# Laying SBUF out anew: stationary tiles beside the constants, weights and work tiles at the other end

## The chip, the cores and the metric

The program runs on one core of one Trainium2 chip. The metric is the device time of one execution in microseconds (us), the median of the runs shown. TensorE does the matrix products, VectorE (DVE), ScalarE (ACT) and GpSimd (POOL) the rest, and DMAs that SyncE (SP) issues bring the weights from HBM into SBUF, the on-chip memory of 128 partitions. A matrix product reads two operands from SBUF: the stationary one (128 columns here) is loaded into the array by an instruction of its own, the moving one (up to 512 columns) is streamed past it. The result goes to PSUM.

## The reference

A decoder of two layers on x of 256 tokens x 1024 channels, all in float32. Each layer does

```
x = x + 0.5 * ((silu(a) * b) @ wo),  a, b = split(rms_norm(x, g) @ wi)      # FFN 1, D_FF = 2816
h = rms_norm(x, g);  z = h @ w_in                                          # queries, keys, values, gates
y = sum over 3 attentions of sigmoid(gate_i) * (o_i @ P_i)                 # stick-breaking, latent, sparse
x = x + y @ w_out
x = x + 0.5 * swiglu_ffn(x)                                                # FFN 2
```

The three attentions have eight heads of width 64 each. Every weight is used once for all 256 tokens, so each is read from HBM once.

## The kernel before

**Products.** The tokens are two tiles of 128 (t = 0, 1). Activations are transposed and are the stationary operand, 128 x 128 at a time; the weights are the moving operand, 512 columns at a time (256 and 440 in a few places). To keep float32 accuracy each operand is split in a high and a low part (`split`, lines 524 to 526), and `mm3` (lines 528 to 532) does three products for one: high x high (L530), high activation x low weight (L531), low activation x high weight (L532). The granted names in the trace read `acc<-whi,hThi`: first the moving, then the stationary tile.

**Stages.** `ffn` runs over six column chunks of a and b (the first of 256, five of 512; eight blocks of 128 in depth, both t, three products each), with hT as the stationary operand; then `out_rows` multiplies gT (silu(a)*b transposed; 22 blocks, both t, both halves of the 1024 output columns) by wo. `mixer` does the input projections with hT, the attentions, the merges with the attention outputs oT (`oh`, `ol`) as the stationary operand, and ends in `out_rows` with yT, which lies in hT's slots, times w_out. By these loops one FFN has 480 products of 512 columns and 96 of 256 on hT and 264 on gT; one mixer 528 of 512, 48 of 440 and 48 of 256 columns on hT, 144 on oT, 36 on the latent vectors cT, and 96 on yT.

**Order.** TensorE executes in the order in which the program is written. In the mixer the order of TensorE, VectorE and ScalarE is worked out by a planner (`Planner`, with costs written by hand) before the program is emitted. Elsewhere the framework schedules VectorE, ScalarE and the DMAs. Weights come in slabs: a DMA into `raw` (six buffers), a ScalarE copy to `whi` (L514, in the mixer L817), a VectorE subtraction to `wlo` (L515, L819); four slabs are held.

**Memory.** A tile pool takes its tiles from SBUF in the order of opening, one behind the other in every partition; a pool that closes gives its place to the next one. All four pools `cp` (constants), `sm`, `wp` (weights), `hp` (hT and the large work tiles "hy": x, h, y, mq, mk, nq, nk) lie on the left side, and behind them in turn `fp` (an FFN's gT) and `mp` (a mixer's tiles). Added up from the tile sizes (a tile is rounded up to 32 bytes), in KB of one partition counted from the kernel's first tile:

| tiles | before | after the change |
| --- | --- | --- |
| constants and small tiles; in them zkh, zkl at 8.2 to 10.7 | 0 to 24.9 | 0 to 24.9 |
| whi, wlo, raw | 24.9 to 40.9, to 56.9, to 68.9 | the last 44 KB, from the far end |
| hy, six tiles of 4 KB | 68.9 to 92.9 | the 24 KB before these |
| hThi, hTlo (two of each) | 92.9 to 100.9, to 108.9 | 24.9 to 32.9, to 40.9 |
| FFN: gh0, gl0, gh1, gl1, 11 KB each | 109.0 to 153.0 | 41.0 to 85.0 |
| mixer: V0, V1, then cT/zw | 109.0 to 125.0, to 133.0 | 41.0 to 57.0, to 65.0 |
| mixer: oh, ol | 139.5 to 147.5, to 155.5 | 65.0 to 73.0, to 81.0 |
| mixer: wr (moving operand of the value products) | 194.2 to 206.2 | 126.2 to 138.2 |

`g_col` in `cp` has 32 bytes, so that before the change the weights, hT, gT, oT and wr all start 32 bytes off a multiple of 64 bytes.

Of the kernel before, what the change touches and what calls it, by code (L numbers as in the profile page):

```python
# [345 lines left out]
W_BUFS = 4  # L346
# [10 lines left out]
def decoder_trunk(ctx, tc, x_in, wts, gains, lcon, cst, out, depth=DEPTH):  # L357
# [3 lines left out]

    cp = ctx.enter_context(tc.tile_pool(name="cp", bufs=1))
    sm = ctx.enter_context(tc.tile_pool(name="sm", bufs=5))
    wp = ctx.enter_context(tc.tile_pool(name="wp", bufs=W_BUFS))
    hp = ctx.enter_context(tc.tile_pool(name="hp", bufs=2))
    dp = ctx.enter_context(tc.tile_pool(name="dp", bufs=1, space=bass.MemoryType.DRAM))
    pb = ctx.enter_context(tc.tile_pool(name="pb", bufs=8, space=PSUM))
    ctx.enter_context(tc.manual_schedule(engines={nc.tensor.engine}))
# [8 lines left out]
        return pb.tile([128, 512], F, tag="ps", name="att")  # L377

    def big_tile(name, dt=F, shape=(128, D)):
        return hp.tile(list(shape), dt, tag="hy", name=name, bufs=6)  # L380

    A = slice(None)

# [5 lines left out]
    for t in range(NT):  # L389
        xs.append(big_tile("x"))  # L390
# [13 lines left out]


    g_row = big_tile("grow")[0:8, 0:128]
    nc.sync.dma_start(g_row, gains[0].rearrange("(k p) -> k p", k=8))
    g_col = cp.tile([128, 8], F, name="g_col")
# [11 lines left out]
    def load_consts():  # L420
        nc.sync.dma_start(ct, cst[:, RW + 128:])
        rf = big_tile("rf")
        nc.sync.dma_start(rf[:, :RW], cst[:, :RW])
        nc.vector.tensor_copy(rt, rf[:, :RW])
# [314 lines left out]
    def mixer(l):  # L739
# [26 lines left out]
        def new_oT():  # L766
            return (mp.tile([128, 4, S], R, tag="oh", name="oh", bufs=2),
                    mp.tile([128, 4, S], R, tag="ol", name="ol", bufs=2))
# [14 lines left out]
        def events(*n):  # L783
            return [events(*n[1:]) for _ in range(n[0])] if n else event()
# [87 lines left out]

        cT = mp.tile([128, 2, NT, 3, 128], R, tag="r3", name="cT")
        cT = cT[:, 0], cT[:, 1]
        krg = [mp.tile([128, 56], F, name=f"krg{t}") for t in range(NT)]
        ev_hT, ev_rn, ev_cT, ev_krg = events(2), [Tok(2.0), Tok(4.0)], events(NT), events(NT)

# [208 lines left out]
        side = {"_uq": side_uq, "_ukv": side_ukv, "w1_slab": lambda: compress()}  # L1086
# [105 lines left out]
                yield from merge(c, *gs[c], o_nsa, ev_onsa, False, final=True)  # L1192


        o_sb, o_mla, o_nsa = new_oT(), new_oT(), new_oT()
        ev_osb, ev_omla, ev_onsa = events(4), events(4), events(4)
        ev_sbpv, ev_sbm = event(), event()

# [318 lines left out]
        def compress():  # L1517

            c = done_c[0]
            done_c[0] += 1  # L1520
            for s in range(2):
                i = take()
                k = yield "P", 1.0, 1.2, (ev_zw, *slab_ev[i]), () if s else (s_acc,)
                if not s:
                    a = acc_tile()
                sl = slabs[i][1]
                for j in range(8):
                    jj = s * 8 + j
                    js = slice(j * 128, (j + 1) * 128)
                    if jj:  # L1530
                        nc.tensor.matmul(a[:M, 0:128], zw[:, c, jj, 0:M], sl[1][:, js], start=False, stop=False)
                    nc.tensor.matmul(a[:32 + M, 0:128], zw[:, c, jj, 0:32 + M], sl[0][:, js],
                                     start=jj == 0, stop=jj == 15)
                    if not jj:
                        nc.tensor.matmul(a[:M, 0:128], zw[:, c, jj, 0:M], sl[1][:, js], start=False, stop=False)
                s_w.put(k)
                mark()
            spawn(hidden(c, a, k), 0.0)
# [252 lines left out]
    for l in range(depth):  # L1791
        ffn(l, 0)
        mixer(l)
        ffn(l, 2)
# [33 lines left out]
```

## Time and profile before

| what | us |
| --- | --- |
| median of 3 runs | 1328.75 (1328.41 to 1329.15) |
| the profiled execution's own time | 1328.05 |
| its span in the profile | 1326.3 |
| TensorE busy in it | 1302.1 |
| VectorE busy | 893.9 |
| ScalarE busy | 796.4 |

In the profile TensorE's products are pipelined and their ends are modelled: one starts before the one ahead of it is shown as ended, and the busy time of a stretch does not tell how fast they follow each other. The views that list instructions in order of time give each one's start; the difference of two starts, divided by the number of products between them, is the spacing that counts for the time. "PEclk" is the TensorE clock that was granted, 1.00 or a digit 9 for its upper level of 2.4 GHz, half for 1.2 GHz.

### The profile page before, as it was taken

The page shows a single profiled execution, that of the slowest core. Times are in us where ns is not written, and L with a number is a line of the kernel's source. Part 1 is how long each engine was busy: PE and PEld are TensorE (multiplying, and loading weights), DVE is VectorE, ACT ScalarE, POOL GpSimd, SP SyncE. Part 2 cuts the span into 40 slices and gives each one's busy share as a digit, 9 for nine tenths or more (in the row PEclk, how much of TensorE's full clock was granted, in tenths as well). Part 3 has the DMA queues.
Part 4 walks back from the last instruction along what each step waited for, and adds up shares of the span by engine and source line. Part 5 has one row for each costly group of instructions (what it writes and reads, how often), then busy time and mean ns, then how long its engine had stood idle before and what let it go on. Part 6 is the DMA issues. An engine that isn't in the chain of part 4 may idle for free.

```text
span 1326.3 us, 19987 instructions
## 1 busy us (share of the span) xinstructions
PE 1302.1 (98%) x6623; PEld 1078.1 (81%) x6623; DVE 893.9 (67%) x1852; ACT 796.4 (60%) x1654; POOL 43.4 (3%) x50
## 2 busy tenths in 40 slices
PE   7999999999899999999999999999989999999998
PEld 6888888888777888888888888888878778888887
DVE  6655557988997775555466554679879876755553
ACT  5545447796888555454464544478868884645442
POOL 0000000210000000000000000011100000000000
PEclk9999999999999999999999999999999999999999
DMA  7765557545434656555656565565453356565563
GB/s 226 245 190 177 189 179 219 181 127 175 128 90 135 184 174 198 189 183 183 191 179 216 178 190 181 188 217 160 133 173 110 102 159 176 173 191 183 183 189 112
DMA packets 124504, 230.77 MB, mean 174 GB/s; under 512 B 13928, under 2 KB 15600, under 8 KB 124400
## 3 DMA queue, kind: packets, MB, share of 16 engines
q1 hardware_dynamic: 124144, 228.97, 55.5%
q8 instruction: 52, 0.85, 0.3%
q0 software_dynamic: 256, 0.52, 0.1%
q14 instruction: 52, 0.43, 0.1%
HBM read 225.77 MB, written 3.15 MB: 173 GB/s over the span
## 4 chain that ended last, share of the span: by engine, by line
PE 85%; ACT 7%; DVE 6%; issue 2%; DMA 0%; SPq 0%; ACTq 0%; DVEq 0%
PE acc L530 26%; PE acc L532 26%; PE acc L531 26%; ACT wf L1340 2%; ACT whi L817 2%; PE tp L692 1%; DVE wlo L819 1%; ACT wf L1367 1%; DVE wr L1384 1%; DVE wlo L515 1%; DVE x L626 1%; PE att L1290 1%; PE att L1726 1%; PE att L1262 1%; DVE wf L1350 0%
## 5 line engine op out<-in xcount | busy, mean ns | idle before, releaser
L515 DVE TENSOR_TENSOR wlo<-raw,whi 128x512 fp32r<-128x512 f32 (+1 forms) x560 | 361.9, 687 | 318.0 <-ACT whi L514 316.6
L514 ACT ACTIVATE whi<-raw 128x512 fp32r<-128x512 f32 (+1 forms) x560 | 323.0, 623 | 374.7 <-PE acc L532 366.4
L530 PE MATMUL acc<-whi,hThi 128*128 128x512 f32 (+2 forms) x1248 | 480.3, 385 | 0.5 <-ACT hThi L525 0.5
L532 PE MATMUL acc<-whi,hTlo 128*128 128x512 f32 (+2 forms) x1248 | 470.4, 377 | 0.6 <-DVE hTlo L526 0.6
L531 PE MATMUL acc<-wlo,hThi 128*128 128x512 f32 (+2 forms) x1248 | 469.0, 376 | 0.0
L532 PEld LDWEIGHTS acc<-whi,hTlo 128*128 128x128 f32 x1248 | 235.3, 189 | 44.6 <-DVE hTlo L526 1.0
L530 PEld LDWEIGHTS acc<-whi,hThi 128*128 128x128 f32 x1248 | 235.7, 189 | 39.5 <-ACT hThi L525 1.0
L531 PEld LDWEIGHTS acc<-wlo,hThi 128*128 128x128 f32 x1248 | 235.9, 189 | 37.7
L819 DVE TENSOR_TENSOR wlo<-raw,whi 128x512 fp32r<-128x512 f32 (+1 forms) x276 | 181.4, 681 | 42.2 <-ACT whi L817 40.6
L817 ACT ACTIVATE whi<-raw 128x512 fp32r<-128x512 f32 (+1 forms) x276 | 162.9, 618 | 53.9 <-PE acc L532 42.4
L530 PE MATMUL acc<-whi,gh 128*128 128x512 f32 x352 | 140.1, 398 | 0.0
L532 PE MATMUL acc<-whi,gl 128*128 128x512 f32 x352 | 139.0, 395 | 0.0
L531 PE MATMUL acc<-wlo,gh 128*128 128x512 f32 x352 | 139.0, 395 | 0.0
L532 PEld LDWEIGHTS acc<-whi,gl 128*128 128x128 f32 x352 | 66.1, 188 | 15.9
L531 PEld LDWEIGHTS acc<-wlo,gh 128*128 128x128 f32 x352 | 66.2, 188 | 15.3
L530 PEld LDWEIGHTS acc<-whi,gh 128*128 128x128 f32 x352 | 66.1, 188 | 15.3
L537 POOL TENSOR_TENSOR rs<-ss,mh 128x1 f32<-128x1 f32 (+4 forms) x30 | 36.6, 1223 | 1034.0 <-DVE ss L536 1012.6
L1340 ACT ACTIVATE wf<-wf,mn 128x128 f32<-128x128 f32 x96 | 42.7, 446 | 12.1 <-DVE mn L1350 11.7
L530 PE MATMUL acc<-whi,oh 128*128 128x512 f32 x96 | 41.2, 429 | 0.5 <-DVE y L1155 0.5
L532 PE MATMUL acc<-whi,ol 128*128 128x512 f32 x96 | 39.1, 408 | 0.0
L531 PE MATMUL acc<-wlo,oh 128*128 128x512 f32 x96 | 39.1, 407 | 0.0
L683 DVE SCALAR_TENSOR_TENSOR g<-acc,rn,sil 128x512 f32<-128x512 f32 (+1 forms) x48 | 33.6, 703 | 2.9 <-PE acc L532 0.8
(274 smaller groups left out, 1262.6 us busy)
## 6 DMA issues: line engine op xcount, KB each, us to landing
raw<-in_wts SPq DMA_DIRECT2D x824, 256.0 KB, 2.7
gain<-in_gains SPq DMA_DIRECT2D x5, 512.0 KB, 5.7
xd<-x SPq DMA_DIRECT2D x4, 512.0 KB, 4.4
x<-xd SPq DMA_DIRECT2D x4, 512.0 KB, 4.1
raw<-in_wts SPq DMA_DIRECT2D x8, 184.0 KB, 2.5
lc<-in_lcon SPq DMA_DIRECT2D x2, 528.0 KB, 7.5
x<-in_x SPq DMA_DIRECT2D x4, 256.0 KB, 5.3
out_dram<-x SPq DMA_DIRECT2D x4, 256.0 KB, 2.0
```

The source lines that it names most:

```text
L514: nc.scalar.activation(hi[:, c:c + m], raw[:, :m], AF.Copy)
L515: nc.vector.tensor_tensor(lo[:, c:c + m], raw[:, :m], hi[:, c:c + m], op=OP.subtract)
L530: nc.tensor.matmul(o, a[0], b[0], start=start, stop=False)
L531: nc.tensor.matmul(o, a[0], b[1], start=False, stop=False)
L532: nc.tensor.matmul(o, a[1], b[0], start=False, stop=stop)
L537: nc.gpsimd.tensor_tensor(r[:p, :w], ss[:p, :w], mh[:p, :w], op=OP.pow)
L626: nc.vector.scalar_tensor_tensor(xv, accs[t, c], 0.5, xv, op0=OP.mult, op1=OP.add)
L683: nc.vector.scalar_tensor_tensor(g[:, :fn], b[:, :fn], rn[t][:, 0:1], s[:, :fn], op0=OP.mult, op1=OP.mult)
L692: nc.tensor.transpose(tp[:, j * 128:(j + 1) * 128], g[:, j * 128:(j + 1) * 128], ident)
L817: nc.scalar.activation(hl[0][:, c:c + m], raw[:, :m], AF.Copy)
L819: nc.vector.tensor_tensor(hl[1][:, c:c + m], raw[:, :m], hl[0][:, c:c + m], op=OP.subtract)
L1340: nc.scalar.activation(E[i][:, cs], E[i][:, cs], AF.Exp, scale=-1.0, bias=mn[:, q:q + 1], accum_out=su[:, q:q + 1])
```

## The change

The weight pool goes to the right side of SBUF (it grows down from the far end), and the large work tiles leave `hp` for a pool `yp` of their own beside it, with the same six buffers. hT, and then gT or the mixer's tiles, so move down to the constants. In the mixer the three oT pairs (six tiles on four buffers, as before) are taken earlier, so that they lie behind cT. No computation and no loop is changed.

```diff
     sm = ctx.enter_context(tc.tile_pool(name="sm", bufs=5))
-    wp = ctx.enter_context(tc.tile_pool(name="wp", bufs=W_BUFS))
     hp = ctx.enter_context(tc.tile_pool(name="hp", bufs=2))
+
+    wp = ctx.enter_context(tc.tile_pool(name="wp", bufs=W_BUFS, side="right"))
+    yp = ctx.enter_context(tc.tile_pool(name="yp", bufs=6, side="right"))
...
     def big_tile(name, dt=F, shape=(128, D)):
-        return hp.tile(list(shape), dt, tag="hy", name=name, bufs=6)
+        return yp.tile(list(shape), dt, tag="hy", name=name)
...
         cT = cT[:, 0], cT[:, 1]
+        o_sb, o_mla, o_nsa = new_oT(), new_oT(), new_oT()
         krg = [mp.tile([128, 56], F, name=f"krg{t}") for t in range(NT)]
...
-        o_sb, o_mla, o_nsa = new_oT(), new_oT(), new_oT()
         ev_osb, ev_omla, ev_onsa = events(4), events(4), events(4)
```

## Rows read from the trace of the kernel before

**Rows 1.** The page: busy time by engine, and the granted clock in 40 slices.
```profile
PE 1302.1 (98%) x6623; PEld 1078.1 (81%) x6623; DVE 893.9 (67%) x1852; ACT 796.4 (60%) x1654; POOL 43.4 (3%) x50
...
PEclk9999999999999999999999999999999999999999
```

**Rows 2.** The page: the chain that ended last, by engine.
```profile
PE 85%; ACT 7%; DVE 6%; issue 2%; DMA 0%; SPq 0%; ACTq 0%; DVEq 0%
```

**Rows 3.** Groups by line and shape: count, busy us, mean ns, idle before and releaser.
```profile
L530 PE MATMUL acc<-whi,hThi 128*128 128x512 f32 x1056 | 421.5, 399 | 0.0
...
L515 DVE TENSOR_TENSOR wlo<-raw,whi 128x512 fp32r<-128x512 f32 x556 | 360.0, 688 | 318.0 <-ACT whi L514 316.6
L514 ACT ACTIVATE whi<-raw 128x512 fp32r<-128x512 f32 x556 | 321.4, 624 | 374.7 <-PE acc L532 366.4 <-DMA raw<-in_wts 4.3 <-issue 3.2
...
L530 PE MATMUL acc<-whi,gh 128*128 128x512 f32 x352 | 140.1, 398 | 0.0
...
L530 PE MATMUL acc<-whi,hThi 128*128 128x256 f32 x160 | 46.8, 293 | 0.5 <-ACT hThi L525 0.5
...
L530 PE MATMUL acc<-whi,oh 128*128 128x512 f32 x96 | 41.2, 429 | 0.5 <-DVE y L1155 0.5
...
L1161 DVE TENSOR_TENSOR y<-y,th 128x512 f32<-128x512 f32 x16 | 11.0, 686 | 0.1
```

**Rows 4.** Busy time in three stretches of the first mixer: PE, PEld, DVE, ACT, POOL.
```profile
201.00:323.00 122.00, 121.96 (x650) 104.23 (x649) 104.65 (x216) 93.60 (x192) 17.51 (x14) 1.00 0.59 179
323.00:434.00 111.00, 104.83 (x662) 83.75 (x661) 92.63 (x281) 92.39 (x255) 0.61 (x1) 0.98 0.42 126
434.00:466.00 32.00, 32.00 (x149) 26.00 (x148) 22.68 (x37) 16.37 (x29) 0.00 (x0) 1.00 0.56 168
```

**Rows 5.** The same stretch 323 to 434: products of L532 alone (PE, PEld).
```profile
323.00:434.00 111.00, 37.91 (x102) 19.37 (x101) 0.98 0.42 126
```

**Rows 6.** Products in order of time (start us, length us), first FFN, hT; 46 apart.
```profile
126.98 0.39 PE L530 MATMUL acc<-whi,hThi 128*128 128x512 f32 x1
...
137.40 0.39 PE L531 MATMUL acc<-wlo,hThi 128*128 128x512 f32 x1
```

**Rows 7.** The same view, first FFN, gT; 196 products apart.
```profile
150.36 0.40 PE L532 MATMUL acc<-whi,gl 128*128 128x512 f32 x1
...
196.10 0.40 PE L530 MATMUL acc<-whi,gh 128*128 128x512 f32 x1
```

**Rows 8.** The same view, w_out on yT in hT's slots; 44 products apart.
```profile
463.12 0.39 PE L532 MATMUL acc<-whi,hTlo 128*128 128x512 f32 x1
...
473.09 0.39 PE L531 MATMUL acc<-wlo,hThi 128*128 128x512 f32 x1
```

**Rows 9.** The same view, the last merge on oT; 24 products apart.
```profile
441.94 0.40 PE L530 MATMUL acc<-whi,oh 128*128 128x512 f32 x1
...
447.54 0.40 PE L530 MATMUL acc<-whi,oh 128*128 128x512 f32 x1
```

**Rows 10.** The same view, 256 columns on hT; 24 products apart.
```profile
20.59 0.28 PE L530 MATMUL acc<-whi,hThi 128*128 128x256 f32 x1
...
23.48 0.28 PE L530 MATMUL acc<-whi,hThi 128*128 128x256 f32 x1
```

**Rows 11.** The same view, 256 columns on zkh and zkl, moving nq; 7 products apart.
```profile
373.71 0.28 PE L531 MATMUL acc<-nq,zkh 128*128 128x256 f32 x1
...
374.51 0.28 PE L532 MATMUL acc<-nq,zkl 128*128 128x256 f32 x1
```

**Rows 12.** The same view, values V stationary, moving wr; 2 products apart.
```profile
433.73 0.40 PE L1743 MATMUL acc<-wr,V 128*128 128x512 f32 x1
...
434.20 0.28 PE L1745 MATMUL acc<-wr,V 128*64 128x256 f32 x1
```

**Rows 13.** The same view, 128 columns of weights on zw; 29 products apart.
```profile
326.38 0.22 PE L1531 MATMUL acc<-wlo,zw 128*30 128x128 f32 x1
...
328.12 0.22 PE L1532 MATMUL acc<-whi,zw 128*62 128x128 f32 x1
```

## The prediction

> **What bounds the kernel now.** I read the busy times first: TensorE works through 98% of the span, VectorE 67%, ScalarE 60%, and the clock is at its upper level in every slice [rows 1]. The chain of waits says the same of the end: 85% of it is TensorE [rows 2]. Then the groups by line: ScalarE, which makes whi (L514), stood idle 374.7 us, 366.4 of them until TensorE's L532 had released a slab; VectorE's L515 waited 316.6 us for that ScalarE copy [rows 3]. So in the FFNs the slabs are ready and wait for their buffers, and TensorE sets the pace. What shortens one product there shortens the run; a faster VectorE or ScalarE would not.
>
> The mixer has to be read by stretches [rows 4]. From 201 to 323 us and from 434 to 466 us TensorE is busy all the time (121.96 of 122.00, 32.00 of 32.00). From 323 to 434 it is busy 104.83 of 111.00, VectorE 92.63, ScalarE 92.39: softmax and sigmoid work there shares the path.
>
> Last, since the change moves only tiles, I looked for anything that differs by a tile's place. Busy times hide it, as the modelled ends overlap; starts in order of time show it. At 2.4 GHz 512 columns take 512 / 2.4 = 213.3 ns, 256 take 106.7 and 128 take 53.3. What a spacing has beyond that I call the pause:
> - hT, 512 columns: 137.40 - 126.98 = 10.42 us over 46 products, 226.5 ns, pause 13.2 [rows 6]. yT in hT's slots: 9.97 over 44, 226.6 [rows 8].
> - gT, 512 columns: 45.74 over 196, 233.4, pause 20.0 [rows 7]. oT: 5.60 over 24, 233.3, pause 20.0 [rows 9].
> - V, with wr moving: 0.47 over 2, 235, about gT's [rows 12].
> - hT, 256 columns: 2.89 over 24, 120.4, pause 13.7 [rows 10].
> - zkh and zkl, 256 columns: 0.80 over 7, 114.3, pause 7.6 [rows 11]. zw, 128 columns: 1.74 over 29, 60.0, pause 6.7 [rows 13].
>
> The pause does not go with the number of columns (512 and 256 on hT have the same) nor with the loop (w_out runs `out_rows` as wo does, and has hT's pause in hT's slots). It goes with the stationary tile's place: small at 8 to 11 KB, twice that at 93 to 109, three times that from 109 up. Its unit is about 6.7 ns (16 cycles). zw breaks the order: it lies above 109 KB with one unit, but these products are so short that something else may set them.
>
> **The change part by part.** *hT, from 93-109 to 25-41 KB.* On it run 480 + 96 products per FFN, 528 + 48 + 48 per mixer, and yT's 96. No row shows a stationary tile of this kind between 11 and 93 KB, so I bound it. Below: the pause of zk, one unit less, or no pause at all, two units less. Above: gT's pause, one unit more. I take one unit less, 6.67 ns, as the new place is nearer to zk's (some 20 KB off) than to the old one (68).
>
> *gT, from 109-153 to 41-85; oT, from 139-155 to 65-81; cT likewise.* Bounds: no gain, or no pause at all, three units less. I take one unit less, to hT's old pause, since their new place lies just below hT's old one.
>
> *The weights, to the far end.* Does a moving operand far up cost more? wr moves from 194-206 KB with V stationary at 109-125, and its spacing is that of gT with weights at 25-57 [rows 7, 12]. So I cost it at nothing; its price if wrong stands under the rivals. A second reading leads to the same sum: the moving tiles start 32 bytes off a multiple of 64, so each product touches one more 64-byte piece than it must, and 64 bytes of the stream are 213.3 / 32 = 6.67 ns. From the far end, with sizes of whole KB, weights start on a multiple.
>
> *VectorE and ScalarE.* I cost their reads and writes at the new places at nothing: L515 on 512 columns in the weights' place takes 688 ns, L1161, of the same shape, in other places 686 [rows 3]. Were each of the 556 L515 10 ns longer, the 316.6 us of waiting in front of them would cover the 5.6 us.
>
> *oT taken earlier.* Taking a tile emits no instruction; the same six tiles share four buffers in the same order. Pools and their buffers stay as many, so no wait is added or removed, and no DMA moves past a queue. Nothing is queued behind anything new.
>
> *The sum.* In the FFNs (four): 512 columns on hT 4 x 480 = 1920, 256 columns 4 x 96 = 384, on gT 4 x 264 = 1056; w_out 2 x 96 = 192. Together 3552, at 6.67 ns 23.7 us. In a mixer the projections and merges are 528 + 48 + 48 + 144 + 36 = 804 products, 268 triples. In 323 to 434 stand 102 products of L532 [rows 5], of which I count 79 on hT or oT (the rest are attention work). The other 189 triples, 567 products, lie where TensorE sets the pace: 2 x 567 x 6.67 = 7.6 us. The 79 triples, 237 products, save 2 x 237 x 6.67 = 3.2 us of TensorE's time; in that stretch it has 6 us of gaps and two other engines are 83% busy, so I credit 0.4 of it, 1.3 us (bounds 0 and 3.2). Sum: 23.7 + 7.6 + 1.3 = 32.6. If slabs come due earlier by 3%, ScalarE and VectorE still have hundreds of us of waiting; the next thing late would be VectorE in the middle of the mixer, which the 0.4 allows for.
>
> The profiled execution took 1328.05 us (span 1326.3 and 1.75 around it), 0.7 below the median of 1328.75. So 1328.05 - 32.6 = 1295.5, plus 0.7: 1296.
>
> A rule of the Trainium skill speaks against all of this. Its page "SBUF — State Buffer", section "Who interferes with whom", gives TensorE one read port for the moving and one for the stationary operand, independent of each other and of all other engines, and says that "PE and ACT never wait on anyone". By that rule a tile's place costs nothing and the time stays 1328.75. The trace does not agree: 226.5 against 233.4 ns for products alike in all but the tiles [rows 6, 7].
>
> **The rivals.** *Two steps.* gT and oT fall by two units, to zk's pause, as hT does. 1056 more units in the FFNs (7.0 us) and 2 x 144 in the merges, not all of them at the full price (some 1.5): about 8.5 less, 1287. For it: by zk, everything below some height may have one unit. Against: nothing between 11 and 93 KB is seen.
>
> *Only gT and oT fall.* If the smallest pause belongs to the first KBs, or to the hy slots that zk's products have as moving operand, hT stays at 226.5. Then 1056 units, 7.0, and about 1.5 in the mixers: 8.5, so 1320.
>
> *Place is not what counts.* The starts modulo 512 bytes differ too: counted from the kernel's first tile's own address, hT's lie 32 bytes off a multiple, gT's 160, oT's 96. These hardly change, and if they set the pause and the moving tile's start does nothing, the change does not do what it says: 1328.75. For it: the pause jumps between neighbours, hT's last slot and gT's first. Against: V, in gT's place, and oT, at another remainder, share gT's value.
>
> *Slower: distance between the operands.* The pause may grow with how far the stationary tile lies from the moving one, each step at a boundary between them. For it: gT is farther from the weights (52 KB and more) than hT (36 and more), and has more. Against: zk and nq are some 60 KB apart with the least. After the change hT and its weights are over 120 KB apart, and gT's over 95. If hT then takes gT's pause, one unit on hT's and yT's products: 1920 + 384 + 192 = 2496 in FFNs and w_out, 16.6 us; in the mixers 2 x 624 less the middle's share, some 900, 6.0 us; 1328.75 + 22.6 = 1351. It decides from the point where hT's spacing at 512 columns is above 226.5.
>
> **How the numbers follow.** The forecast has a chance of 0.44, with a range of its own of 1288 to 1304 (the middle stretch's bounds and a quarter unit on the 4,700 products). Two steps 0.12; only gT and oT 0.14; place does not count 0.14; distance 0.16. A measurement of this kernel tells 0.2%, 2.7 us, from no change. Faster are the first three, 0.70; within it 0.14; slower 0.16. The range is to leave out two in ten: 1280 takes in the two steps with a few us to spare (no pause at all on hT would be lower, and is left out), and 1331 takes in "place does not count"; the distance case and a rest stay outside.
>
> **What would show it.** Right: after the change hT's spacing at 512 columns is 220 ns and gT's and oT's 226.7, zk's as before; the stretch in the middle of the mixer shrinks by less than 3%, the FFNs by about 3%; L515's and L514's means stay at 688 and 624. gT at 220 is the two-step case; hT at 226.5 with gT below 233 the third; both unchanged the fourth. Wrong altogether: hT at 233 or more, or spacings that fall while the span does not, which would mean that a wait of the slabs has come to the path, to be seen as idle time of TensorE before L530 with ScalarE's L514 as the releaser.

## The result, and the profile after

The changed kernel takes 1337.89 us (median of 4 runs, 1337.15 to 1339.73), before 1328.95 in the same comparison: ratio 1.0069, 95% interval 1.0051 to 1.0086. It is slower by 9 us, where 33 us less had been forecast, and it lies above the range.

The page of the changed kernel: busy time by engine, the granted clock, and the chain. Its lines are numbered two higher in `mm3` than before (L532 to L534 for L530 to L532).

```profile
PE 1311.8 (98%) x6623; PEld 1076.9 (81%) x6623; DVE 893.8 (67%) x1852; ACT 796.5 (60%) x1654; POOL 42.3 (3%) x50
...
PEclk9999999999899999999999999999999999999999
...
PE 84%; ACT 7%; DVE 6%; issue 2%; DMA 0%; SPq 0%; DVEq 0%; ACTq 0%
```

Against [rows 1, 2] only one thing has moved: TensorE is busy 9.7 us longer with the same 6623 products. The span grew by 9.5 (1326.3 to 1335.8). VectorE, ScalarE and the chain's shape are as before. So no new wait has come; the products themselves follow each other more slowly. One slice of the clock row reads 8 (334 to 367 us, the middle of the first mixer); the stretches whose spacings are read below lie in slices that read 9.

The groups of the changed kernel that answer to [rows 3]:

```profile
L532 PE MATMUL acc<-whi,hThi 128*128 128x512 f32 x1056 | 426.4, 404 | 0.0
...
L517 DVE TENSOR_TENSOR wlo<-raw,whi 128x512 fp32r<-128x512 f32 x556 | 360.0, 688 | 323.1 <-ACT whi L516 322.1
L516 ACT ACTIVATE whi<-raw 128x512 fp32r<-128x512 f32 x556 | 321.3, 625 | 380.8 <-PE acc L534 370.1 <-DMA raw<-in_wts 5.3 <-issue 3.3
...
L532 PE MATMUL acc<-whi,hThi 128*128 128x256 f32 x160 | 46.1, 288 | 0.5 <-ACT hThi L527 0.5
```

VectorE's subtraction (688 ns, as before) and ScalarE's copy (625, was 624) take no longer with the weights at the far end. Products on hT are shown longer at 512 columns (399 to 404 ns) and shorter at 256 (293 to 288): the same tiles, moved once, and two answers. A price that goes by height alone does not give that.

The same products in order of time as in [rows 6 to 11], in the changed kernel (start us, length us): hT at 512 columns, gT, yT in w_out, oT, hT at 256 columns, zkh and zkl.

```profile
129.07 0.39 PE L532 MATMUL acc<-whi,hThi 128*128 128x512 f32 x1
...
139.81 0.39 PE L533 MATMUL acc<-wlo,hThi 128*128 128x512 f32 x1
...
152.59 0.39 PE L534 MATMUL acc<-whi,gl 128*128 128x512 f32 x1
...
197.46 0.39 PE L532 MATMUL acc<-whi,gh 128*128 128x512 f32 x1
...
467.06 0.39 PE L534 MATMUL acc<-whi,hTlo 128*128 128x512 f32 x1
...
477.33 0.39 PE L533 MATMUL acc<-wlo,hThi 128*128 128x512 f32 x1
...
445.83 0.40 PE L532 MATMUL acc<-whi,oh 128*128 128x512 f32 x1
...
451.43 0.40 PE L532 MATMUL acc<-whi,oh 128*128 128x512 f32 x1
...
20.43 0.28 PE L532 MATMUL acc<-whi,hThi 128*128 128x256 f32 x1
...
23.26 0.28 PE L532 MATMUL acc<-whi,hThi 128*128 128x256 f32 x1
...
377.32 0.28 PE L533 MATMUL acc<-nq,zkh 128*128 128x256 f32 x1
...
378.16 0.28 PE L534 MATMUL acc<-nq,zkl 128*128 128x256 f32 x1
```

With the counts of the rows before (46, 196, 44, 24, 24 and 7 products), the spacings are as follows. The rows are rounded to 0.01 us, which leaves some 0.2 ns over 46 products and over 1 ns over 7.

| products | before, ns | after, ns | start past the moving tile's, bytes modulo 512, before | after |
| --- | --- | --- | --- | --- |
| hT, 512 columns | 226.5 | 233.5 | 0 | 64 |
| yT in hT's slots, 512 | 226.6 | 233.4 | 0 | 64 |
| gT, 512 | 233.4 | 228.9 | 128 | 192 |
| oT, 512 (last merge) | 233.3 | 233.3 | 64 | 192 |
| hT, 256 | 120.4 | 117.9 | 0 | 64 |
| zkh and zkl, 256 | 114.3 | 120.0 | 64 or 192 modulo 256 | 128 or 0 modulo 256 |

The last two columns are the experiments' subject: the stationary operand's start address less the moving one's, added up from the tile sizes. zk is read at four offsets (columns 32, 0, 128 and 96), so it has two distances. By the sizes hT's and gT's own starts are the same modulo 512 as before and oT's is 64 bytes further on; the weights, which now count from the far end, start 64 bytes lower modulo 512. The far end's address itself stands in no run; that the 64 bytes are right, modulo 256, is seen below in e4 and e8, which undo and make them by tile sizes alone.

Two rows of the table need care. zk's do not hold: there are only twelve such products in a mixer, and in the kernel before the same seven gaps of the second mixer, on the same tiles, give 118.6 ns:

```profile
1029.55 0.28 PE L531 MATMUL acc<-nq,zkh 128*128 128x256 f32 x1
...
1030.38 0.28 PE L532 MATMUL acc<-nq,zkl 128*128 128x256 f32 x1
```

And hT's 24 products of 256 columns and oT's 24 are not typical of the changed kernel: over all stretches of six products the median of hT at 256 columns is 113.3 ns after (120.0 before), that of oT 229.0 after (233.3 before). To oT's the section on e4 comes back.

Where the 9.5 us stand, by the starts of the same products in both traces:

| stretch | before, us | after, us |
| --- | --- | --- |
| first product to first gT product (FFN's 576 products on hT) | 134.59 | 137.06 |
| gT, first to last product, first FFN | 63.06 | 61.98 |
| first mixer, and the next FFN's hT | 403.20 | 408.36 |
| third FFN's hT | 126.40 | 128.69 |
| second mixer, and the last FFN's hT | 403.34 | 407.36 |

The four hT phases and the mixers add up to 13.9 us more, gT's four to 4.3 less. In the first FFN 480 x 6.67 - 96 x 6.67 = 2.6 us were to come from hT by the spacings; 2.5 came.

The mixer's stretches of the changed kernel, between the same products as those of [rows 4] to within two (PE, PEld, DVE, ACT, POOL):

```profile
202.25:325.58 123.33, 123.27 (x650) 103.85 (x649) 104.97 (x216) 93.99 (x193) 16.96 (x14) 1.00 0.56 178
325.58:437.66 112.08, 106.13 (x660) 84.46 (x659) 92.38 (x281) 92.30 (x255) 0.61 (x1) 0.97 0.40 125
437.66:470.10 32.44, 32.44 (x150) 26.04 (x149) 22.71 (x37) 16.40 (x29) 0.00 (x0) 1.00 0.51 164
```

Each is longer by about what TensorE's busy time grew (1.3, 1.3 and 0.4 us); VectorE and ScalarE did the same work.

### The profile page after: what moved, and what is told of

Same layout as the page of the kernel before. It is cut to its first block, busy times and chain, and to the rows that moved or that the text cites. A ratio compares the mean times of both kernels' runs of the same rounds, so it can differ in the third digit from the quotient of the medians.

```text
span 1335.8 us, 19987 instructions
## 1 busy us (share of the span) xinstructions
PE 1311.8 (98%) x6623; PEld 1076.9 (81%) x6623; DVE 893.8 (67%) x1852; ACT 796.5 (60%) x1654; POOL 42.3 (3%) x50
## 4 chain that ended last, share of the span: by engine, by line
PE 84%; ACT 7%; DVE 6%; issue 2%; DMA 0%; SPq 0%; DVEq 0%; ACTq 0%
PE acc L532 26%; PE acc L534 26%; PE acc L533 26%; ACT wf L1342 2%; ACT whi L819 2%; PE tp L694 1%; DVE wlo L821 1%; ACT wf L1369 1%; DVE wr L1386 1%; DVE wlo L517 1%; DVE x L628 1%; PE att L1292 1%; PE att L1728 1%; PE tp L1378 1%; PE att L1264 1%
## 5 line engine op out<-in xcount | busy, mean ns | idle before, releaser
L532 PE MATMUL acc<-whi,hThi 128*128 128x512 f32 (+2 forms) x1248 | 484.4, 388 | 0.5 <-ACT hThi L527 0.5
L534 PE MATMUL acc<-whi,hTlo 128*128 128x512 f32 (+2 forms) x1248 | 473.9, 380 | 0.4 <-DVE hTlo L528 0.2
L534 PEld LDWEIGHTS acc<-whi,hTlo 128*128 128x128 f32 x1248 | 235.0, 188 | 49.5 <-DVE rn L576 0.4
L532 PEld LDWEIGHTS acc<-whi,hThi 128*128 128x128 f32 x1248 | 235.3, 189 | 44.4 <-ACT hThi L527 1.0
L533 PEld LDWEIGHTS acc<-wlo,hThi 128*128 128x128 f32 x1248 | 235.5, 189 | 42.3
L532 PE MATMUL acc<-whi,gh 128*128 128x512 f32 x352 | 139.8, 397 | 0.0
L534 PE MATMUL acc<-whi,gl 128*128 128x512 f32 x352 | 138.1, 392 | 0.0
L534 PEld LDWEIGHTS acc<-whi,gl 128*128 128x128 f32 x352 | 66.1, 188 | 15.4
L532 PEld LDWEIGHTS acc<-whi,gh 128*128 128x128 f32 x352 | 66.2, 188 | 12.7
L532 PE MATMUL acc<-whi,oh 128*128 128x512 f32 x96 | 41.7, 434 | 0.4 <-DVE y L1158 0.4
L534 PE MATMUL acc<-whi,ol 128*128 128x512 f32 x96 | 39.1, 407 | 0.0
```

The lines of the kernel that those rows point to most:

```text
L532: nc.tensor.matmul(o, a[0], b[0], start=start, stop=False)
L533: nc.tensor.matmul(o, a[0], b[1], start=False, stop=False)
L534: nc.tensor.matmul(o, a[1], b[0], start=False, stop=stop)
```

## The experiments

**Theory 1:** the pause is set by the distance of the two operands' start addresses modulo some hundred bytes. **Theory 2,** the prediction's: height in SBUF or distance in KB. The first three kernels shift gT alone, by another amount in each of the four FFNs, so that one profile reads four distances.

**e1, e2, e3: gT shifted by bytes.**

```diff
             fp = es.enter_context(tc.tile_pool(name="fp", bufs=2))
+            pad = FPADS[2 * l + (gi != 0)]     # e1 (320, 448, 256, 128); e2 (32768, 352, 96, 384)
+            if pad:                            # e3, in the kernel before: (384, 64, 192, 320)
+                fp.tile([128, pad // 4], F, name="pad", bufs=1)
```

> The changed kernel, with an unused tile of 320, 448, 256 and 128 bytes ahead of gT in the four FFNs, so that gT starts 0, 128, 448 and 320 bytes beyond the weights modulo 512. Theory 1 (the pause is set by the distance of the two operands' start addresses modulo 512 bytes): gT's spacing at 512 columns differs between the FFNs; 0 gives 226.7 ns, as hT had before the change, 128 gives 233.3, as gT had; 448 and 320 are not known. Theory 2 (height in SBUF or distance in KB): all four stay at the changed kernel's 228.8 ns.

> The changed kernel, with an unused tile of 32768, 352, 96 and 384 bytes ahead of gT in the four FFNs: 192, 32, 288 and 64 bytes beyond the weights modulo 512, the first one 32 KB higher in SBUF. Theory 1 (distance modulo 512 bytes): 228.8 ns in the first FFN in spite of the 32 KB, 233.3 in the last (64, as hT has after the change and oT had before it); 32 and 288 are not known. Theory 2 (height, or distance in KB): the first FFN, nearer to the weights and higher, moves away from 228.8 by up to one unit of 6.7 ns, the other three stay at 228.8.

> The kernel before, with an unused tile of 384, 64, 192 and 320 bytes ahead of gT in the four FFNs: 0, 192, 320 and 448 bytes beyond the weights modulo 512. Theory 1 (distance modulo 512): gT goes from 233.3 ns to 226.7 in the first FFN and to 228.8 in the second, and the last two show what the changed kernel shows at 320 and 448. If the two addresses count each by itself and not their distance, these four values do not match those of the changed kernel at the same distance. Theory 2 (height in SBUF): all four stay at 233.3.

One execution of each: 1339.91, 1339.90 and 1325.99 us. The spacing is read as in [rows 7], over the same 196 products of each FFN. e1, first FFN (distance 0) and last (320):

```profile
152.29 0.39 PE L535 MATMUL acc<-whi,gl 128*128 128x512 f32 x1
...
196.73 0.39 PE L533 MATMUL acc<-whi,gh 128*128 128x512 f32 x1
...
1284.32 0.39 PE L535 MATMUL acc<-whi,gl 128*128 128x512 f32 x1
...
1330.05 0.39 PE L533 MATMUL acc<-whi,gh 128*128 128x512 f32 x1
```

44.44 / 196 = 226.7 ns and 45.73 / 196 = 233.3. e2, first FFN, 32 KB higher with the distance unchanged:

```profile
152.48 0.39 PE L535 MATMUL acc<-whi,gl 128*128 128x512 f32 x1
...
197.34 0.39 PE L533 MATMUL acc<-whi,gh 128*128 128x512 f32 x1
```

44.86 / 196 = 228.9: 32 KB change nothing. e3, the kernel before, first FFN, distance 0, at 109 KB and up:

```profile
151.41 0.39 PE L533 MATMUL acc<-whi,gl 128*128 128x512 f32 x1
...
195.86 0.39 PE L531 MATMUL acc<-whi,gh 128*128 128x512 f32 x1
```

44.45 / 196 = 226.8. e3's second FFN (192) has 228.9, the third (320) 233.3, the fourth (448) 228.9: each is what the changed kernel shows at the same distance, though both addresses differ. Theory 2 falls; it is the distance that counts, not either address by itself. (whi, wlo and raw have the same remainders in every run, so that it is the moving tile whose start counts, and not raw's beside it, is argued and not shown.)

**e5, e6: the other eight distances.** The same pads, in the kernel of e4 below, of 416, 480, 32, 64 and of 160, 192, 224, 288 bytes.

> The kernel of e4, with an unused tile of 416, 480, 32 and 64 bytes ahead of gT: 96, 160, 224 and 256 bytes beyond the weights modulo 512. Theory 1 (distance modulo 512) has no values for these; by the neighbours measured so far (64: 233.3 ns, 128: 232.5, 192: 228.8, 288: 233.3) they lie between 226.7 and 233.3. Theory 2 (the number of places that fit, not the distance): 228.8 in all four.

> The kernel of e4, with an unused tile of 160, 192, 224 and 288 bytes ahead of gT: 352, 384, 416 and 480 bytes beyond the weights modulo 512. Theory 1: between 226.7 and 233.3 ns (neighbours: 320: 233.3, 448: 228.8, 0: 226.7; V on wr at 384 about 233); a value below 226.7 would be a better place than any so far.

1327.16 and 1329.46 us, one execution of each. e5's last FFN (distance 256) is the one that stands out, 44.44 / 196 = 226.7 ns:

```profile
1272.99 0.39 PE L536 MATMUL acc<-whi,gl 128*128 128x512 f32 x1
...
1317.43 0.39 PE L534 MATMUL acc<-whi,gh 128*128 128x512 f32 x1
```

All sixteen, ns at 512 columns:

| distance | 0 | 32 | 64 | 96 | 128 | 160 | 192 | 224 |
| --- | --- | --- | --- | --- | --- | --- | --- | --- |
| spacing | 226.7 to 226.9 | 233.3 | 233.3 | 234.2 | 232.4 to 233.3 | 233.4 | 228.9 | 233.3 |
| distance + 256 | 226.7 | 233.3 | 233.3 | 234.2 | 233.3 | 233.4 | 228.9 | 233.3 |

The second row repeats the first: what counts is the distance modulo 256 bytes. None is below 226.7. At 128 the runs differ: 233.3 in the kernel before and in e7, 232.4 in e1's second FFN.

**e4: hT alone lowered by 64 bytes.**

```diff
     hp = ctx.enter_context(tc.tile_pool(name="hp", bufs=2))
+    cq = ctx.enter_context(tc.tile_pool(name="cq", bufs=1))
...
-    mh = cp.tile([128, 16], F, name="mh")
+    mh = cq.tile([128, 16], F, name="mh")
```

> The changed kernel, with one constant of 64 bytes (mh) laid behind hT instead of ahead of it: hT starts 64 bytes lower, 0 beyond the weights modulo 512 as before the change; everything else keeps its place. Theory 1: hT's spacing at 512 columns goes from 233.3 back to 226.7 ns, at 256 columns from 113.3 to 120; about 3000 products of 512 columns in the stretches that TensorE paces give 20 us back, 480 of 256 take 3: about 1321 us, faster than both kernels. Theory 2 (height, or distance in KB): 64 bytes do nothing, 1338 us.

1324.5 us, ratio to before 0.9962 (0.9950 to 0.9974): 13 us below the changed kernel by the place of one constant, though 3.5 above the estimate, which had put too many of the mixers' products at full price: without the FFNs' hT the two mixers and w_out give back some 4 us in the trace, where the estimate has nearly 7. Against before, hT's terms cancel and gT's 4.3 us are left: 1328.7 - 4.3 = 1324.4. hT's rows, 512 columns (46 products) and 256 (24):

```profile
127.80 0.39 PE L533 MATMUL acc<-whi,hThi 128*128 128x512 f32 x1
...
138.23 0.39 PE L534 MATMUL acc<-wlo,hThi 128*128 128x512 f32 x1
...
21.37 0.28 PE L533 MATMUL acc<-whi,hThi 128*128 128x256 f32 x1
...
24.25 0.28 PE L533 MATMUL acc<-whi,hThi 128*128 128x256 f32 x1
```

10.43 / 46 = 226.7 and 2.88 / 24 = 120.0: both back to [rows 6, 10], the one better and the other worse.

The same kernel shows that a tile's own distance is not all. oT has not moved (distance 192 as in the changed kernel), and of its last merge the same 24 products as in [rows 9] are

```profile
441.60 0.39 PE L533 MATMUL acc<-whi,oh 128*128 128x512 f32 x1
...
447.10 0.39 PE L533 MATMUL acc<-whi,oh 128*128 128x512 f32 x1
```

5.50 / 24 = 229.2 ns, where the changed kernel has 233.3. The products just ahead of them, on hT, follow each other at 226.7 here and at 233.3 there. e1 and e2 repeat the one value, e5 and e6 the other. So in a short stretch the spacing also hangs on what ran just before; how, stays open.

**e7: the new places with the old distances.** e4, with `pad = 448` ahead of gT in every FFN, and the oT pairs taken at their old point (oT's distance is 128 then, for 64 before; zk keeps the changed kernel's).

> The kernel of e4 (hT 0 bytes beyond the weights modulo 512, as before the change) with 448 bytes ahead of gT (128 beyond, as before) and the oT pairs taken at their old point (128 beyond; before the change 64): weights, work tiles, hT and gT lie where the change puts them, but all distances modulo 512 have the spacing of before. Theory 1 (only the distance modulo 512 counts): spacings of 226.7, 120, 232.5 to 233.3, and 1328 us, the time of before. Theory 2 (the move by tens of KB costs or gives something of its own): the time differs from 1328 by over 3 us.

1328.66 us against 1328.28, ratio 1.0005 (0.9995 to 1.0014). hT and gT, in time:

```profile
126.07 0.39 PE L534 MATMUL acc<-whi,hThi 128*128 128x512 f32 x1
...
136.50 0.39 PE L535 MATMUL acc<-wlo,hThi 128*128 128x512 f32 x1
...
149.46 0.40 PE L536 MATMUL acc<-whi,gl 128*128 128x512 f32 x1
...
195.19 0.40 PE L534 MATMUL acc<-whi,gh 128*128 128x512 f32 x1
```

226.7 and 233.3 ns, as in [rows 6, 7]. Moving the weights, the work tiles, hT and gT by some 70 to 140 KB costs and gives nothing that can be measured; the interval leaves room for under 2 us.

**e8: the old places with nearly the new distances.**

```diff
     wp = ctx.enter_context(tc.tile_pool(name="wp", bufs=W_BUFS))
+    qp = ctx.enter_context(tc.tile_pool(name="qp", bufs=1))
+    qp.tile([128, 16], F, name="pad")
     hp = ctx.enter_context(tc.tile_pool(name="hp", bufs=2))
```

> The kernel before, with an unused tile of 64 bytes between the weights and hT: hT 64 bytes beyond the weights modulo 512, gT 192, oT 128 (the changed kernel has 64, 192, 192); no tile is moved by more. Theory 1: hT 233.3 ns at 512 columns and 113.3 at 256, gT 228.8, and about 1338 us, as slow as the changed kernel. Theory 2 (height or distance in KB): 1328.7 us.

1337.06 us against 1328.28, ratio 1.0070 (1.0049 to 1.0090), the changed kernel's 1.0069. hT and gT:

```profile
129.20 0.39 PE L532 MATMUL acc<-whi,hThi 128*128 128x512 f32 x1
...
139.93 0.39 PE L533 MATMUL acc<-wlo,hThi 128*128 128x512 f32 x1
...
152.72 0.39 PE L534 MATMUL acc<-whi,gl 128*128 128x512 f32 x1
...
197.58 0.39 PE L532 MATMUL acc<-whi,gh 128*128 128x512 f32 x1
```

233.3 and 228.9 ns. hT's 256 columns, 24 products, 2.72 / 24 = 113.3:

```profile
20.70 0.28 PE L532 MATMUL acc<-whi,hThi 128*128 128x256 f32 x1
...
23.42 0.28 PE L532 MATMUL acc<-whi,hThi 128*128 128x256 f32 x1
```

An empty tile of 64 bytes makes the whole of the loss. The work tiles move along with hT here, so their distance to it does not count. Nor is it the clock: with 0.999 granted this kernel takes 1335.5 us, and the kernel before with 1.000 took 1326.1 and 1328.0. e7 and e8 together settle the cause from both sides.

**e9: every distance from the weights 0.** The changed kernel, with the small tiles mh and rn taken from ahead of hT and gT to the far end.

```diff
     yp = ctx.enter_context(tc.tile_pool(name="yp", bufs=6, side="right"))
+    cq = ctx.enter_context(tc.tile_pool(name="cq", bufs=1, side="right"))
...
-    mh = cp.tile([128, 16], F, name="mh")
+    mh = cq.tile([128, 16], F, name="mh")
...
-        q = hp.tile([128, 3], F, tag="rn", name="rn", bufs=4)
+        q = cq.tile([128, 3], F, tag="rn", name="rn", bufs=4)
```

> The changed kernel, with the constant mh and the four small rn tiles (192 bytes) taken from ahead of hT and gT to a pool at the far end: hT, gT, oT, cT all start 0 beyond the weights modulo 512. By the distance theory every product of 512 columns on them takes 226.7 ns, 256 columns 120: against e4 (1324.5 us) gT's 1056 products and the merges' 288 win 2.1 ns each, 2.8 us: about 1321.7 us, the fastest so far, 0.5% below before. If places a few hundred bytes away do not add up like this, it stays near 1324.5.

1321.68 us against 1328.71, ratio 0.9951 (0.9937 to 0.9965): faster than both kernels, by the sum that the spacings gave. gT, and oT:

```profile
149.53 0.40 PE L535 MATMUL acc<-whi,gl 128*128 128x512 f32 x1
...
193.99 0.39 PE L533 MATMUL acc<-whi,gh 128*128 128x512 f32 x1
...
439.78 0.39 PE L533 MATMUL acc<-whi,oh 128*128 128x512 f32 x1
...
445.22 0.39 PE L533 MATMUL acc<-whi,oh 128*128 128x512 f32 x1
```

44.46 / 196 = 226.8 and 5.44 / 24 = 226.7.

**e10: the same, and every start a multiple of 64 bytes.** e9, with g_col (32 bytes) in a pool at the far end, opened ahead of the weights.

> e9, with the 32 bytes of g_col taken to the far end too: all distances stay 0, but weights and stationary tiles now start on multiples of 64 bytes instead of 32 beyond one. If only the distance counts: as e9, 226.7 ns and about 1321.7 us. The prediction's second reading (a moving tile off a multiple of 64 costs one unit): 220.0 ns on the 4,700 products that count, 31 us less, about 1291 us.

1322.35 us, ratio 0.9955 (0.9943 to 0.9968), not to be told from e9. hT:

```profile
127.22 0.39 PE L534 MATMUL acc<-whi,hThi 128*128 128x512 f32 x1
...
137.65 0.39 PE L535 MATMUL acc<-wlo,hThi 128*128 128x512 f32 x1
```

10.43 / 46 = 226.7, not 220: that both operands start on a multiple of 64 bytes gains nothing, and the piece of 64 bytes was a wrong reading.

**e11: high and low part at different distances.** e9, with pads between gh and gl.

```diff
+            dh, dl = HILO[2 * l + (gi != 0)]   # (0, 64), (64, 0), (0, 128), (0, 32): gh and gl
+            # a pad of (d - d of the tile before) % 512 bytes ahead of each of the four tiles
```

> e9, with gh and gl (the high and the low part of gT) at different distances from the weights: (gh, gl) at (0, 64), (64, 0), (0, 128), (0, 32) bytes in the four FFNs. Each tile's own distance counts: in the first FFN the spacing differs by the part whose tile is loaded, and the mean of the three products lies between 226.7 and 233.3, nearer to 226.7 where gh (two of three products) is at 0. If the state is one for the whole sequence and the worst tile sets it: 233.3 in all four.

1324.97 us, one execution. First FFN, (0, 64), and last, (0, 32):

```profile
150.22 0.40 PE L536 MATMUL acc<-whi,gl 128*128 128x512 f32 x1
...
195.51 0.39 PE L534 MATMUL acc<-whi,gh 128*128 128x512 f32 x1
...
1269.38 0.39 PE L536 MATMUL acc<-whi,gl 128*128 128x512 f32 x1
...
1315.10 0.40 PE L534 MATMUL acc<-whi,gh 128*128 128x512 f32 x1
```

231.1 and 233.3 ns; (64, 0) and (0, 128) have 231.2 and 231.1. Neither expectation holds: gl off 0, read by one product of three, costs as much as gh off 0, read by two, so it is not a mean by products, and three of the four stay below 233.3, so the worst does not rule either. Nor does the loss stay with one product. In the first FFN the gap behind a product on gl is the long one (235.5 ns, against 228.4 and 229.3); in the last, where again gl alone is off 0, it is the shortest (228.0, against 231.9 and 239.9). How the distance acts in detail stays open.

## Why the prediction was wrong

**What failed is the step from the spacings to their cause: the pause was read as a price of height, one unit of 6.67 ns for each step up.** That spacings differ by the stationary tile was right, and that this would decide the time. The prediction read "small at 8 to 11 KB, twice that at 93 to 109, three times that from 109 up". The upper two rungs were also 0 bytes (hT) and 64 or 128 bytes (oT, gT) past the moving tile. The lowest was no rung: it rested on seven gaps of zk's, at 64 and 192 bytes modulo 256, and the second mixer of the same trace has 118.6 ns there for 114.3. The rival that named addresses modulo 512 was put at 0.14 and at no change, because "these hardly change" and on the condition that "the moving tile's start does nothing". That looked at each stationary tile's own remainder. e3 against e1 shows that the distance counts, and the weights moved by 64 bytes modulo 512 under tiles that kept their own.

**Step by step.** hT: forecast 6.67 ns less, measured 6.7 more; on hT's and yT's 2112 products of the FFNs and w_out a forecast of -14 us became +14. gT: forecast 6.67 less, measured 4.5 less. Products of 256 columns: 6.67 less (113.3 for 120.0), as forecast but for another reason, and so by luck: e4 takes it back by 64 bytes. By these spacings the sum's 23.7 us less for the FFNs and w_out come out at some 7 more. The mixers' 8.9 less came out at some 3 more: their two rows in the table of stretches grew by 9.2 us, of which 4.6 are the next FFN's hT and 1.3 w_out. The rows held the warning: zw, which "breaks the order", and the jump from hT's last slot to gT's first, which no height explains.

**The weights' far end.** Costed at nothing for its place, which e7 bears out. The second reading leant on their starting on a multiple of 64 there. They do not: 64 bytes lower than a start that is 32 off such a multiple is 32 off again. And e10, where they do, gains nothing.

**What held.** VectorE's and ScalarE's durations, no new wait, no cost of the oT pairs' new point beyond the distance that it gives them. The prediction also named how the opposite outcome would look, "hT at 233 or more": that is what came. The rival tied to it, distance in KB at 1351 us, had the sign but not the cause: in e7 the operands are as many KB apart as in the changed kernel, at 226.7 ns. Its sum charged hT one unit without the 256 columns' gain or gT's.

The two spacings of one tile at one height bear on a rule of the Trainium skill, whose page "SBUF — State Buffer", section "Who interferes with whom", has TensorE's two read ports independent and says that "PE and ACT never wait on anyone". Taken so, 64 empty bytes between the operands' tiles should cost nothing; they cost TensorE 9 us (e8). That the streaming operand and the next load meet somewhere is one explanation; no run here shows where the time is lost.

## What to carry to other kernels

When a kernel is bound by products that read both operands from SBUF, read the spacing of their starts and set it beside the start addresses of both tiles modulo small powers of two, before any reading by kilobytes. A pad of 32 to 224 bytes in a pool then tests it at next to no cost in memory. Read a long run of products for it: here twelve in a row misled. A change of layout moves these remainders for every tile behind it, so two layouts can be compared only with the distances held equal, as e7 does.

## What the runs showed of the hardware that was not expected

- Products of 512 columns (fp32r, 128 x 128 stationary, a weight load for each) follow each other at 226.7 to 226.9 ns over 196 products when the stationary tile starts 0 bytes past the moving one modulo 256, at 228.9 for 192 and at 232 to 234 for the other six multiples of 32 (before, after, e1 to e3, e5, e6).
- Products of 256 columns on hT go the other way: 120.0 ns at 0 (before, e4), 113.3 at 64 (e8).
- The distance does not fix the spacing of a short stretch. The same oT products at distance 192 take 233.3 ns behind hT's at 233.3 (after, e1, e2) and 229 behind hT's at 226.7 (e4 to e6).
- A few products in a row do not tell the spacing. Ten products after transposes in the kernel before, on hT, still took 235, 233, 236, 224, 231, 236, 228, 232, 231 and 227 ns (start to start, from 124.44 us) before 226 to 227 became steady; in the changed kernel 236 and 230 or 231 alternate through the whole stretch.
